# The first stage of a hybrid decoder trunk: x in its own places, the second half by blocks, the rotary tables early

## The chip, the core and the metric

The kernel runs on one core of a Trainium2 chip. The metric is the time of one execution on the device in microseconds, as a median of several runs; lower is better. The core has TensorE (matrix products, PE in the rows), VectorE (DVE), ScalarE (ACT), GpSimd (POOL), and SyncE (SP), whose queue issues all DMAs here. Each takes its instructions in a fixed order and waits on semaphores.

## The reference

Two layers over 1024 tokens of width 1024. The first layer's mixer begins with an RMS norm and one input projection; 512 of its columns go to a causal pooling (two groups of 128 channels, and their gates), the others to six heads of differential attention with a partial rotary embedding.

```python
hn = rmsnorm(h, norm_g[i])
z = hn @ w_in
a_in, a_gate, q, k, v, b_gate = split(z)
a = multiscale_pool(a_in)          # trailing means over 2, 4, 8, 16 tokens, minus the token
a = einsum(a, pool_w) * pool_scale * silu(a_gate)
q = partial_rope(rmsnorm(q, q_norm), positions, 16, 500000.0)     # k likewise
o = diff_attention(q, k, v, lam)
h = h + concat([a, o]) @ w_out
```

The second layer has latent attention and a gated delta rule. Each layer ends with a gated addition of per-layer inputs. All of that is the same before and after.

## The kernel before, in words

Activations lie transposed: 8 blocks k of 128 channels, 2 halves h of 512 tokens. To multiply float32 at the fast rate each operand is split into a rounded high part and a low rest (`split`, L131); a product is then three matmuls (`mm3`, L141, lines L142, L143, L144). The norm's gain `ng` scales x as it is split (L137 on ScalarE for the high part, L138 on VectorE for the low one); the norm's 1/rms comes in later, as a row over tokens (`rrow`).

The first stage (L343 to L366) loads x and the pooling's 512 weight columns. `load_x` (L312) takes one x block into a raw buffer (four raw buffers serve x and weights alike), splits it, and lets ScalarE square it and GpSimd add the squares (L322). The first half is multiplied block by block into four PSUM banks; the weights are rounded on VectorE (L349) and the rest is taken there (L350). Then the constants are loaded, `finish_x` (L324) makes 1/rms: column sums on TensorE (L182), a root by Newton steps on VectorE (L111 to L116), a row by a product with ones (`token_row`, L185, operand at L187, product L190, copy L191). `pool_in` (L334) takes the banks out. After it the second half's eight x blocks are loaded and split, and multiplied column block by column block. The rotary tables (`rope_tables`, L193; called at L370) are a chain of some 60 small VectorE operations (L207 to L227), two sines on ScalarE (L228) and copies on GpSimd.

Then come the projections of head 0 (`even_proj`, L433; weights split on ScalarE L134 and VectorE L135) and between them the pooling (`even_pool`, L407): shifted sums on GpSimd (L411), and on VectorE, for each half of the partitions, a scaling and subtraction (L422 to L424). Its product is L428.

The code is written in a program order, but a scheduler decides at build time in which order each engine's queue holds the instructions; it lets work that is ready early move ahead. Before the change it had moved much of the tables' chain between the first half and the last three x blocks. Pools of tiles with a tag hand out their buffers in turn; an instruction that needs a buffer still in use waits.

Of the kernel before, what the change touches and what calls it, by code (L numbers as in the profile page):

```python
# [10 lines left out]
F32 = mybir.dt.float32  # L11
F32R = mybir.dt.float32r
I32 = mybir.dt.int32
# [8 lines left out]
P = 128  # L22
# [34 lines left out]
def trunk_kernel(ctx, tc, a, out, layers=2):  # L57
# [11 lines left out]
    def nm(p):  # L69
        uid[0] += 1  # L70
        return f"{p}{uid[0]}"
# [76 lines left out]
        dma.dma_start(raw, src)  # L148
        return raw

    def wload(ap, c0, n, nk=KC):

        res = []
        for k in range(nk):
            raw = wp.tile([P, 512], F32, tag="raw", bufs=4, name=nm("raw"))[:, :n]
            hi = wp.tile([P, 512], F32R, tag="hi", name=nm("wh"))[:, :n]
            lo = wp.tile([P, 512], F32R, tag="lo", name=nm("wl"))[:, :n]
            dma.dma_start(raw, ap[k * P:(k + 1) * P, c0:c0 + n])
            split(hi, lo, raw)
            res.append((hi, lo))  # L160
        return res
# [31 lines left out]
    def rope_tables(pool, lo, n, tmp, tab=None):  # L193
# [1 line left out]

        posi = pool.tile([P, NT], I32, name=nm("posi"))
        dma.dma_start(posi, a["positions"].rearrange("b (t p) -> p (b t)", p=P))
        posf = pool.tile([P, NT], F32, name=nm("posf"))  # L200
        v.tensor_copy(posf, posi)
        ct, st = [(tab or pool.tile)([P, NT, 2 * n], F32, name=nm(i)) for i in ("cos", "sin")]
        acc = st.rearrange("p t n -> p (t n)")[:, 0:NT * n]
        fr = ct.rearrange("p t n -> p (t n)")[:, 0:NT * n]
# [100 lines left out]
    yp = pools["sm"] = pools["y"]  # L305
    PW, PBUFS = [T_ + 16], {0: 2, 1: 1}

    ng = vec(cp, "ng", a["norm_g"].rearrange("l (c p) -> p (l c)", p=P), 16)
    hn = [[None, None] for _ in range(KC)]
    rrow = [T("g", 3) for _ in range(2)]  # L310

    def load_x(h, k, sums):  # L312
        raw = stage(a["xT"][k * P:(k + 1) * P, h * 512:(h + 1) * 512])
        hi, lo = xt(), xt()
        split(hi, lo, raw, ng[:, k:k + 1])
        hn[k][h] = (hi, lo)
        if k == 0:
            s.activation(sums, raw, AF.Square)
        else:
            sq = T("z", 2)  # L320
            s.activation(sq, raw, AF.Square)
            g.tensor_tensor(out=sums, in0=sums, in1=sq, op=ALU.add)  # L322
# [17 lines left out]
        s.activation(th, ag, AF.Tanh, scale=0.5)  # L340
        v.scalar_tensor_tensor(out=ag, in0=th, scalar=1.0, in1=ag, op0=ALU.add, op1=ALU.mult)

    sums = T("o", 2)  # L343
    first, w_pool = [bank(n) for n in ("acc", "acc", "s", "s")], []
    for k in range(KC):
        load_x(0, k, sums)
        raw = stage(a["ev_w_in"][k * P:(k + 1) * P, 0:512])
        hi, lo = [wp.tile([P, 512], F32R, tag=n, name=nm(n)) for n in ("hi", "lo")]
        v.tensor_copy(hi, raw)  # L349
        v.tensor_tensor(out=lo, in0=raw, in1=hi.bitcast(F32), op=ALU.subtract)  # L350
        w_pool.append((hi, lo))
        for j in range(4):
            q = slice(j * P, j * P + P)
            mm3(first[j], hi[:, q], lo[:, q], *hn[k][0], k == 0, k == KC - 1)
    dma.dma_start(cst, a["cst"])
    finish_x(0, sums)
    for j in range(4):
        pool_in(first[j], j, 0)
    sums = T("o", 2)
    for k in range(KC):  # L360
        load_x(1, k, sums)
    finish_x(1, sums)
    for j, n in enumerate(("x", "x", "tr", "acc")):
        ps = bank(n)
        proj_T(hn, w_pool, j, 1, ps)
        pool_in(ps, j, 1)  # L366

    rtmp = T("o", 2, (3, 64))
    rtmp = [rtmp[:, i, :] for i in range(3)]
    cos0, sin0 = rope_tables(yp, 0, 8, lambda dt: rtmp.pop().bitcast(dt),  # L370
                             lambda shape, dt, name: T("pt", 2, shape[1:], dt))
    lvt = T("o", 2)[:, 0:256]
    dma.dma_start(lvt, a["ev_lambda"].rearrange("o a b -> (o a b)").partition_broadcast(P))
    neglam = yp.tile([P, 1], F32, name="neglam")
# [32 lines left out]
    def even_pool(b):  # L407
        x, s2, s4 = px[b], T("p0", 2, (L,)), T("p0", 2, (L,))

        def shift_add(dst, src, sh, lo):  # L410
            g.tensor_tensor(out=dst[lo:P, sh:L], in0=src[lo:P, sh:L], in1=src[lo:P, 0:L - sh], op=ALU.add)  # L411
            g.memset(dst[lo:P, 0:sh], 0.0)

        g.memset(x[:, 0:16], 0.0)
        shift_add(s2, x, 1, 0)
        shift_add(s4, s2, 2, 64 if b == 0 else 0)
        if b == 1:
            shift_add(s2, s4, 4, 0)
            shift_add(s4, s2, 8, 64)
        for sw, lo in ((s2, 0), (s4, 64)):  # L420
            q = slice(lo, lo + 64)
            v.tensor_tensor(out=sw[q, 16:32], in0=sw[q, 16:32], in1=cst[q, C_ICNT + 16 * b:C_ICNT + 16 * b + 16], op=ALU.mult)  # L422
            v.tensor_tensor(out=x[q, 16:32], in0=sw[q, 16:32], in1=x[q, 16:32], op=ALU.subtract)
            v.scalar_tensor_tensor(out=x[q, 32:L], in0=sw[q, 32:L], scalar=cst[q, C_IW + b:C_IW + b + 1],  # L424
                                   in1=x[q, 32:L], op0=ALU.mult, op1=ALU.subtract)
        for h in range(2):
            pm = bank("s")
            pe.matmul(pm, pw[:, b, :], x[:, 16 + 512 * h:528 + 512 * h], start=True, stop=True)  # L428
            ct = T("sq", 3)
            v.scalar_tensor_tensor(out=ct, in0=pm, scalar=pscale[:, b:b + 1], in1=pg[2 * b + h], op0=ALU.mult, op1=ALU.mult)  # L430
            dma.dma_start(cat[0][b][h], ct)
# [883 lines left out]
```

## Time and profile before

| | |
|---|---|
| median of 3 runs (lowest, highest) | 1497.71 us (1496.02, 1498.46) |
| the profiled execution's own time | 1490.0 us |
| its span, first to last instruction | 1488.3 us |
| TensorE busy | 1419.7 us, 95% of the span |
| VectorE busy | 1000.5 us, 67% |
| ScalarE, GpSimd busy | 655.7 us, 44%; 206.2 us, 14% |
| mean granted TensorE clock | 0.99 of full speed |
| DMA | 181.52 MB, 122 GB/s in the mean |

The busy share is a mean over stages. TensorE's slices show 7 in the first and fourth slot and nearly always 9 behind them, so the stage at the start is looked at by itself below. Every time of an instruction is from the one profiled execution.

### The profile page before, as it was taken

To read this page: it belongs to the slowest core of one execution; us is meant where nothing else is said; L and a number is where in the kernel's file an instruction comes from. 1 tells how busy PE (TensorE), PEld (TensorE's weight loads), DVE (VectorE), ACT (ScalarE), POOL (GpSimd) and SP (SyncE) were. 2 spreads that over 40 slices of the span, in tenths; PEclk is the share of its full clock that TensorE was granted. 3 is DMA by queue.
4 is the path that set the end of the run, shared out by engine and by line. 5 is a ranking of instruction groups with operands and counts; after the bars stand their busy time and mean duration, and the time that the engine had idled before them with its cause. 6 is when DMAs were issued, how large, how long until landed. Compare 5 with 4: busy or idle time off the path is not lost. (4 is left out here: it accounts for less than half of the span.)

```text
span 1488.3 us, 22788 instructions
## 1 busy us (share of the span) xinstructions
PE 1419.7 (95%) x7494; PEld 1158.3 (78%) x7494; DVE 1000.5 (67%) x2939; ACT 655.7 (44%) x1642; POOL 206.2 (14%) x347
## 2 busy tenths in 40 slices
PE   7799999999999999999998999999889999999998
PEld 6578887888888778887886777888768788887786
DVE  7855666676767857356669789888577888643342
ACT  4415555565566751234454434444223446722220
POOL 3430101010101001012104441110000000000021
PEclk9999999999999999999999999999989999999999
DMA  5315233232335483334323442343455644353332
GB/s 166 95 51 141 56 101 79 78 90 68 100 86 148 134 276 94 107 120 152 118 41 131 167 154 99 99 133 123 138 162 183 212 140 149 114 156 99 120 114 85
DMA packets 131557, 181.52 MB, mean 122 GB/s; under 512 B 32496, under 2 KB 59248, under 8 KB 131440
## 3 DMA queue, kind: packets, MB, share of 16 engines
q1 hardware_dynamic: 131440, 180.08, 39.7%
q8 instruction: 59, 0.97, 0.3%
q14 instruction: 58, 0.48, 0.1%
HBM read 108.20 MB, written 52.95 MB: 108 GB/s over the span
## 5 line engine op out<-in xcount | busy, mean ns | idle before, releaser
L142 PE MATMUL acc<-wh,x 128*128 128x512 f32 (+1 forms) x576 | 231.6, 402 | 2.3 <-DVE g L454 1.9
L143 PE MATMUL acc<-wl,x 128*128 128x512 f32 (+1 forms) x576 | 229.9, 399 | 3.0 <-DVE wl L135 3.0
L144 PE MATMUL acc<-wh,x 128*128 128x512 f32 (+1 forms) x576 | 228.5, 397 | 0.0
L144 PE MATMUL acc<-x,wl 128*128 128x512 f32 x512 | 204.5, 400 | 3.3 <-DVE wl L135 3.3
L142 PE MATMUL acc<-x,wh 128*128 128x512 f32 x512 | 204.8, 400 | 1.9 <-ACT wh L134 0.9
L143 PE MATMUL acc<-x,wh 128*128 128x512 f32 x512 | 203.0, 397 | 0.0
L134 ACT CAST wh<-raw 128x512 fp32r<-128x512 f32 (+2 forms) x176 | 101.3, 599 | 80.2 <-PE acc L143 25.6
L135 DVE TENSOR_TENSOR wl<-raw,wh 128x512 fp32r<-128x512 f32 (+2 forms) x176 | 114.9, 674 | 28.6 <-ACT wh L134 25.9
L143 PEld LDWEIGHTS acc<-wl,x 128*128 128x128 f32 x576 | 109.4, 190 | 27.1 <-DVE wl L135 4.5
L142 PEld LDWEIGHTS acc<-wh,x 128*128 128x128 f32 x576 | 109.3, 190 | 25.7 <-issue 2.8
L144 PEld LDWEIGHTS acc<-wh,x 128*128 128x128 f32 x576 | 109.2, 190 | 22.3
L144 PEld LDWEIGHTS acc<-x,wl 128*128 128x128 f32 x512 | 96.5, 188 | 27.9 <-DVE wl L135 5.9
L142 PEld LDWEIGHTS acc<-x,wh 128*128 128x128 f32 x512 | 96.4, 188 | 25.0 <-ACT wh L134 1.3
L265 ACT ACTIVATE p<-p,mx 128x128 f32<-128x128 f32 (+7 forms) x128 | 99.4, 777 | 33.0 <-DVE mx L261 24.3
L143 PEld LDWEIGHTS acc<-x,wh 128*128 128x128 f32 x512 | 96.3, 188 | 21.5
L669 POOL TENSOR_TENSOR u<-hp,hp 128x512 f32<-128x512 f32 x32 | 43.5, 1358 | 486.9 <-DVE hp L135 205.7
L144 PE MATMUL acc<-hp,wl 128*128 128x512 f32 x256 | 101.6, 397 | 0.4 <-DVE wl L135 0.4
L143 PE MATMUL acc<-hp,wh 128*128 128x512 f32 x256 | 101.5, 396 | 0.0
L142 PE MATMUL acc<-hp,wh 128*128 128x512 f32 x256 | 101.4, 396 | 0.0
L261 DVE CUSTOM_DVE_ANT_0 p<-s,cst 128x512 f32<-128x512 f32 (+3 forms) x128 | 74.2, 586 | 29.2 <-PE s L523 15.6
L667 DVE SCALAR_TENSOR_TENSOR th<-th,ld 128x512 f32<-128x512 f32 x32 | 28.8, 899 | 73.7 <-ACT th L665 73.7
L450 ACT ACTIVATE z<-acc,rstd 128x256 f32<-128x256 f32 x48 | 22.7, 474 | 112.2 <-PE acc L144 112.2
(462 smaller groups left out, 2906.1 us busy)
## 6 DMA issues: line engine op xcount, KB each, us to landing
raw<-in_ev_w_in SPq DMA_DIRECT2D x56, 256.0 KB
Q<-sq SPq DMA_DIRECT2D x96, 128.0 KB
qkv<-zz SPq DMA_DIRECT2D x16, 640.0 KB
raw<-cat SPq DMA_DIRECT2D x32, 256.0 KB
ple<-z SPq DMA_DIRECT2D x32, 256.0 KB
raw<-in_ple_w_gate SPq DMA_DIRECT2D x32, 256.0 KB
ld<-ple SPq DMA_DIRECT2D x32, 256.0 KB
zq<-qkv SPq DMA_DIRECT2D x16, 512.0 KB
```

The source lines that it names most:

```text
L134: s.copy(hi, src)
L135: v.tensor_tensor(out=lo, in0=src, in1=hi.bitcast(F32), op=ALU.subtract)
L142: pe.matmul(ps, lh, rh, start=first, stop=False)
L143: pe.matmul(ps, lh, rl, start=False, stop=False)
L144: pe.matmul(ps, ll, rh, start=False, stop=last)
L261: v.tensor_tensor_reduce(out=pm[:, c * 512:c * 512 + n], in0=ps[:, 0:n], in1=mk, scale=-scale, scalar=prev, op0=ALU.add, op1=ALU.min, accu ...
L265: s.activation(pm[:, 0:w], pm[:, 0:w], AF.Exp, bias=prev, scale=-1.0, accum_out=sums)
L450: s.activation(z[:, t % 4, :], ps[:, 0:256], AF.Identity, scale=rstd[0][:, t:t + 1])
L667: v.scalar_tensor_tensor(out=th, in0=th, scalar=1.0, in1=r, op0=ALU.add, op1=ALU.mult)
L669: g.tensor_tensor(out=u, in0=hi.bitcast(F32), in1=lo.bitcast(F32), op=ALU.add)
```

## The change

- The gains and the positions are loaded as rows and turned by one transpose into `npos` (128x48), from which `ng` and `posf` are views; the identity part of the constants is loaded first, the rest in two later parts.
- x goes into tiles that later hold head 0's K, V and probabilities (`slots`), not into the raw buffers.
- The weights of the first stage are loaded by `wload`, one block per call, so that the high part is rounded on ScalarE (L134).
- The rotary tables are called in the first half's loop, behind block 1.
- The second half is multiplied block by block into three banks as it is split; the fourth column block follows when a bank of `acc` is free. `finish_x(0)` is called behind block 2, and the banks of the first half are taken out from block 4 on.
- `even_pool` copies the lower 64 partitions to the other tile on ScalarE and then scales and subtracts all 128 at once.

```diff
--- before
+++ after
-    def wload(ap, c0, n, nk=KC):
+    def wload(ap, c0, n, nk=KC, row=0):
         res = []
-        for k in range(nk):
+        for k in range(row, row + nk):
...
-        posi = pool.tile([P, NT], I32, name=nm("posi"))
-        dma.dma_start(posi, a["positions"].rearrange("b (t p) -> p (b t)", p=P))
-        posf = pool.tile([P, NT], F32, name=nm("posf"))
-        v.tensor_copy(posf, posi)
...
-    ng = vec(cp, "ng", a["norm_g"].rearrange("l (c p) -> p (l c)", p=P), 16)
+    dma.dma_start(ident, a["cst"][:, C_ID:C_ID + P])
+    rows, posi = T("rt", 1, (P,)), T("th", 2, (P,), I32)[0:NT]
+    v.memset(rows[0:64], 0.0)
+    dma.dma_start(rows[32:48], a["norm_g"].rearrange("l (c p) -> (l c) p", p=P))
+    dma.dma_start(posi, a["positions"].rearrange("b (t p) -> (b t) p", p=P))
+    v.tensor_copy(rows[0:NT], posi)
+    npos = cp.tile([P, 48], F32, name="npos")
+    ps = bank("tr")
+    pe.transpose(ps[:, 0:64], rows[0:64], ident[0:64, 0:64])
+    v.tensor_copy(npos, ps[:, 0:48])
+    posf, ng = npos[:, 0:NT], npos[:, 32:48]
...
+    slots = [[t[:, i, :] for t in [T("K", 4, (2, 512)) for _ in range(4)] for i in range(2)],
+             [T("v", 4) for _ in range(4)] + [t[:, 512 * i:512 * i + 512] for t in [T("p0", 2, (PW[0],)) for _ in range(2)] for i in range(2)]]
     def load_x(h, k, sums):
-        raw = stage(a["xT"][k * P:(k + 1) * P, h * 512:(h + 1) * 512])
+        raw = slots[h][k]
+        dma.dma_start(raw, a["xT"][k * P:(k + 1) * P, h * 512:(h + 1) * 512])
...
-    sums = T("o", 2)
+    sums = [T("o", 2) for _ in range(2)]
     first, w_pool = [bank(n) for n in ("acc", "acc", "s", "s")], []
     for k in range(KC):
-        load_x(0, k, sums)
-        raw = stage(a["ev_w_in"][k * P:(k + 1) * P, 0:512])
-        hi, lo = [wp.tile([P, 512], F32R, tag=n, name=nm(n)) for n in ("hi", "lo")]
-        v.tensor_copy(hi, raw)
-        v.tensor_tensor(out=lo, in0=raw, in1=hi.bitcast(F32), op=ALU.subtract)
-        w_pool.append((hi, lo))
+        load_x(0, k, sums[0])
+        w_pool += wload(a["ev_w_in"], 0, 512, row=k, nk=1)
         for j in range(4):
             q = slice(j * P, j * P + P)
-            mm3(first[j], hi[:, q], lo[:, q], *hn[k][0], k == 0, k == KC - 1)
-    dma.dma_start(cst, a["cst"])
-    finish_x(0, sums)
-    for j in range(4):
-        pool_in(first[j], j, 0)
-    sums = T("o", 2)
-    for k in range(KC):
-        load_x(1, k, sums)
-    finish_x(1, sums)
-    for j, n in enumerate(("x", "x", "tr", "acc")):
-        ps = bank(n)
-        proj_T(hn, w_pool, j, 1, ps)
-        pool_in(ps, j, 1)
-    rtmp = T("o", 2, (3, 64))
-    rtmp = [rtmp[:, i, :] for i in range(3)]
-    cos0, sin0 = rope_tables(yp, 0, 8, lambda dt: rtmp.pop().bitcast(dt),
-                             lambda shape, dt, name: T("pt", 2, shape[1:], dt))
+            mm3(first[j], w_pool[k][0][:, q], w_pool[k][1][:, q], *hn[k][0], k == 0, k == KC - 1)
+        if k == 1:
+            dma.dma_start(cst[:, C_INVF:C_END], a["cst"][:, C_INVF:C_END])
+            rtmp = T("g", 3, (3, 64))
...
+            cos0, sin0 = rope_tables(yp, 0, 8, ...)
+    second = [bank(n) for n in ("x", "x", "tr")]
+    dma.dma_start(cst[:, P:C_INVF], a["cst"][:, P:C_INVF])
+    for k in range(KC):
+        load_x(1, k, sums[1])
+        for j in range(3):
+            q = slice(j * P, j * P + P)
+            mm3(second[j], w_pool[k][0][:, q], w_pool[k][1][:, q], *hn[k][1], k == 0, k == KC - 1)
+        if k == 2:
+            finish_x(0, sums[0])
+        if k > 3:
+            pool_in(first[k - 4], k - 4, 0)
+    finish_x(1, sums[1])
+    second.append(bank("acc"))
+    proj_T(hn, w_pool, 3, 1, second[3])
     for j in range(4):
+        pool_in(second[j], j, 1)
...
-        for sw, lo in ((s2, 0), (s4, 64)):
-            q = slice(lo, lo + 64)
-            v.tensor_tensor(out=sw[q, 16:32], in0=sw[q, 16:32], in1=cst[q, ...], op=ALU.mult)
-            v.tensor_tensor(out=x[q, 16:32], in0=sw[q, 16:32], in1=x[q, 16:32], op=ALU.subtract)
-            v.scalar_tensor_tensor(out=x[q, 32:L], in0=sw[q, 32:L], scalar=cst[q, ...], in1=x[q, 32:L], ...)
+        s.copy(s4[0:64, 16:L], s2[0:64, 16:L])
+        v.tensor_tensor(out=s4[:, 16:32], in0=s4[:, 16:32], in1=cst[:, ...], op=ALU.mult)
+        v.tensor_tensor(out=x[:, 16:32], in0=s4[:, 16:32], in1=x[:, 16:32], op=ALU.subtract)
+        v.scalar_tensor_tensor(out=x[:, 32:L], in0=s4[:, 32:L], scalar=cst[:, ...], in1=x[:, 32:L], ...)
```

How the scheduler's order moves. First, VectorE's queue where the first half is split; before (`x` are the parts of x, `hi` and `lo` of the weights):

```order
L138 SCALAR_TENSOR_TENSOR x_278<-raw_275,ng,x_277 128x512
L349 CAST hi_286<-raw_284 128x512
L350 TENSOR_TENSOR lo_287<-raw_284,hi_286 128x512
L138 SCALAR_TENSOR_TENSOR x_305<-raw_302,ng,x_304 128x512
L349 CAST hi_313<-raw_311 128x512
L350 TENSOR_TENSOR lo_314<-raw_311,hi_313 128x512
```

and after (`wl` is the low part of a weight block, `g` and `pt` are the tables' work tiles):

```order
L138 SCALAR_TENSOR_TENSOR x_359<-K_172,npos,x_358 128x512
L213 SCALAR_TENSOR_TENSOR pt_241<-g_240 128x64
L135 TENSOR_TENSOR wl_367<-raw_365,wh_366 128x512
L217 TENSOR_TENSOR pt_242<-pt_242,pt_241 128x64
L212 TENSOR_SCALAR g_240<-g_240 128x64
L138 SCALAR_TENSOR_TENSOR x_385<-K_172,npos,x_384 128x512
```

The cast has left the queue, and three operations of the tables stand in each block. Second, TensorE's queue around the first row product L190; before:

```order
L142 MATMUL x_515<-x_456,hi_286 128x512
L143 MATMUL x_515<-x_457,hi_286 128x512
L190 MATMUL o_406<-sq_404,cst 128x512
L144 MATMUL x_515<-x_456,lo_287 128x512
L142 MATMUL x_541<-x_422,hi_178 128x512
```

and after:

```order
L144 MATMUL x_461<-x_557,wl_367 128x512
L190 MATMUL o_536<-sq_534,cst 128x512
L142 MATMUL x_462<-x_557,wh_366 128x512
L143 MATMUL x_462<-x_558,wh_366 128x512
L144 MATMUL x_462<-x_557,wl_367 128x512
```

In both it stands in the second half behind block 4; before, that was within the first column block, and after it is within the loop that multiplies three column blocks at a time; 33 products of that loop stand behind it. Third, VectorE's queue at the head of the first half's root (`tokm` to `newton`), which makes that product's operand; before:

```order
L138 SCALAR_TENSOR_TENSOR x_457<-raw_454,ng,x_456 128x512
L121 TENSOR_SCALAR tokm_389<-o_384 128x4
L207 TENSOR_SCALAR o_625<-cst,posf_628 128x8
L111 TENSOR_SCALAR toky_391<-tokm_389 128x4
L207 TENSOR_SCALAR o_625<-cst,posf_628 128x8
L113 TENSOR_TENSOR newton_392<-toky_391 128x4
```

and after:

```order
L222 TENSOR_TENSOR g_240<-g_240 128x64
L223 TENSOR_SCALAR g_240<-g_240 128x64
L135 TENSOR_TENSOR wl_738<-raw_736,wh_737 128x512
L121 TENSOR_SCALAR tokm_519<-o_514 128x4
L111 TENSOR_SCALAR toky_521<-tokm_519 128x4
L113 TENSOR_TENSOR newton_522<-toky_521 128x4
```

Before, the root began behind the fifth x block of the second half, together with the first step of the tables. After, all eight x blocks, the tables to their end and the first weight block of head 0 stand ahead of it. From the first product of head 0 on, TensorE's order is the same in both.

## Rows read from the trace of the kernel before

**Rows 1.** Windows: us, busy of PE, PEld, DVE, ACT, POOL, clock, DMA, GB/s.

```profile
11.40:32.20 20.80, 20.80 (x91) 16.75 (x90) 19.07 (x23) 9.70 (x17) 8.91 (x6) 1.00 0.65 190
...
47.90:55.10 7.20, 0.36 (x2) 0.00 (x0) 6.92 (x15) 3.08 (x6) 4.58 (x4) 0.81 0.11 34
...
55.10:59.70 4.60, 4.57 (x12) 3.61 (x13) 3.26 (x12) 0.91 (x2) 0.00 (x0) 0.55 0.58 164
...
92.30:97.00 4.70, 4.70 (x14) 3.70 (x15) 1.26 (x3) 0.00 (x0) 0.00 (x0) 0.64 0.30 113
```

**Rows 2.** TensorE's timeline, start: start, duration, instruction, idle before, releaser.

```profile
7.34 0.76 PE L142 MATMUL acc<-x,hi 128*128 128x512 f32 x1 [7.34 <-DVE hi L349]
8.64 0.79 PE L143 MATMUL acc<-x,hi 128*128 128x512 f32 x1 [0.53 <-DVE x L138]
...
9.66 0.63 PE L142 MATMUL acc<-x,hi 128*128 128x512 f32 x1
10.09 0.63 PE L143 MATMUL acc<-x,hi 128*128 128x512 f32 x1
```

**Rows 3.** TensorE's timeline, 28 to 100 us.

```profile
32.18 0.95 PE L182 MATMUL o<-cst,o 128*128 128x1 f32 x8
...
55.13 0.79 PE L143 MATMUL x<-x,hi 128*128 128x512 f32 x1 [6.87 <-DVE x L138]
...
67.39 1.10 PE L190 MATMUL o<-sq,cst 128*128 128x512 f32 x2 [1.77 <-DVE neglam L381]
...
70.88 0.40 PE L142 MATMUL acc<-wh,x 128*128 128x512 f32 x1
...
92.26 0.47 PE L142 MATMUL acc<-wh,x 128*128 128x512 f32 x1 [1.91 <-DVE g L454]
```

**Rows 4.** VectorE's timeline, 20 to 60 us.

```profile
22.10 0.42 DVE L349 CAST hi<-raw 128x512 fp32r<-128x512 f32 x1
...
26.59 1.52 DVE L349 CAST hi<-raw 128x512 fp32r<-128x512 f32 x1
...
28.14 0.69 DVE L350 TENSOR_TENSOR lo<-raw,hi 128x512 fp32r<-128x512 f32 x1
28.75 0.74 DVE L138 SCALAR_TENSOR_TENSOR x<-raw,ng,x 128x512 fp32r<-128x512 f32 x1
...
43.36 1.28 DVE L216 TENSOR_SCALAR o<-o 128x64 int32<-128x64 f32 x1
...
52.72 0.18 DVE L216 TENSOR_SCALAR o<-o 128x64 int32<-128x64 f32 x1
...
53.34 0.19 DVE L216 TENSOR_SCALAR o<-o 128x64 int32<-128x64 f32 x1
...
54.33 0.75 DVE L138 SCALAR_TENSOR_TENSOR x<-raw,ng,x 128x512 fp32r<-128x512 f32 x1
...
55.49 0.75 DVE L138 SCALAR_TENSOR_TENSOR x<-raw,ng,x 128x512 fp32r<-128x512 f32 x1
```

**Rows 5.** VectorE's timeline, the pooling.

```profile
86.16 3.41 DVE L424 SCALAR_TENSOR_TENSOR Q<-p,cst,Q 64x1008 f32<-64x1008 f32 x1
...
89.78 1.27 DVE L424 SCALAR_TENSOR_TENSOR Q<-p,cst,Q 64x1008 f32<-64x1008 f32 x1
```

**Rows 6.** GpSimd's timeline, and its group in 7.31 to 57.4 us (count, busy, mean).

```profile
43.22 9.50 POOL L322 TENSOR_TENSOR o<-o,z 128x512 f32<-128x512 f32 x7 [15.40 <-ACT z L321]
...
L322 POOL TENSOR_TENSOR o<-o,z 128x512 f32<-128x512 f32 x14 | 19.6, 1402 | 31.8 <-ACT z L321 31.4
```

**Rows 7.** ScalarE's and SP's timelines, first stage.

```profile
4.99 1.28 ACT L137 ACT_TABLE_LOAD   x1 [4.99 <-DMA raw<-in_xT]
...
50.60 0.60 ACT L134 CAST wh<-raw 128x512 fp32r<-128x512 f32 x1
...
1.30 1.40 SPq L148 DMA_DIRECT2D raw<-in_xT  x1
```

**Rows 8.** Waits of ScalarE, 0 to 60 us: total, times, longest.

```profile
ACT x L137 <- DMA raw<-in_xT: 13.0, 10, 2.5
```

More of the change, by code (lines that the diff above doesn't have):

```diff
@@ L368, in trunk_kernel @@
-    rtmp = T("o", 2, (3, 64))
-    rtmp = [rtmp[:, i, :] for i in range(3)]
-    cos0, sin0 = rope_tables(yp, 0, 8, lambda dt: rtmp.pop().bitcast(dt),
-                             lambda shape, dt, name: T("pt", 2, shape[1:], dt))
+            mm3(first[j], w_pool[k][0][:, q], w_pool[k][1][:, q], *hn[k][0], k == 0, k == KC - 1)
+        if k == 1:
+            dma.dma_start(cst[:, C_INVF:C_END], a["cst"][:, C_INVF:C_END])
+            rtmp = T("g", 3, (3, 64))
+            rtmp = [rtmp[:, i, :] for i in range(3)]
+            cos0, sin0 = rope_tables(yp, 0, 8, lambda dt: rtmp.pop().bitcast(dt),
+                                     lambda shape, dt, name: T("pt", 2, shape[1:], dt))
@@ L419, in even_pool @@
             shift_add(s4, s2, 8, 64)
-        for sw, lo in ((s2, 0), (s4, 64)):
-            q = slice(lo, lo + 64)
-            v.tensor_tensor(out=sw[q, 16:32], in0=sw[q, 16:32], in1=cst[q, C_ICNT + 16 * b:C_ICNT + 16 * b + 16], op=ALU.mult)
-            v.tensor_tensor(out=x[q, 16:32], in0=sw[q, 16:32], in1=x[q, 16:32], op=ALU.subtract)
-            v.scalar_tensor_tensor(out=x[q, 32:L], in0=sw[q, 32:L], scalar=cst[q, C_IW + b:C_IW + b + 1],
-                                   in1=x[q, 32:L], op0=ALU.mult, op1=ALU.subtract)
+        s.copy(s4[0:64, 16:L], s2[0:64, 16:L])
+        v.tensor_tensor(out=s4[:, 16:32], in0=s4[:, 16:32], in1=cst[:, C_ICNT + 16 * b:C_ICNT + 16 * b + 16], op=ALU.mult)
+        v.tensor_tensor(out=x[:, 16:32], in0=s4[:, 16:32], in1=x[:, 16:32], op=ALU.subtract)
+        v.scalar_tensor_tensor(out=x[:, 32:L], in0=s4[:, 32:L], scalar=cst[:, C_IW + b:C_IW + b + 1],
+                               in1=x[:, 32:L], op0=ALU.mult, op1=ALU.subtract)
         for h in range(2):
```

## The prediction, as it was made before the changed kernel ran

> **What bounds the kernel now.** I read the page first: TensorE is busy for 95% of the span, VectorE for 67%. A stage before the dense part can therefore gain only what TensorE idles or runs slowly in it. Second came the windows over the first 140 us [rows 1]: from 11.4 to 32.2 us TensorE has no gap and takes 20.80/91 = 0.23 us a product of 128x512; from 47.9 to 55.1 us it has work for 0.36 us; after that gap it runs at a granted clock of 0.55 for 4.6 us, with 12 products where 20 would fit at 0.23 us, a loss of 8 x 0.23 = 1.9 us. Third came TensorE's timeline. The first product starts at 7.34 us, the second at 8.64 us; the start runs at the lower level, one product per 10.09 - 9.66 = 0.43 us [rows 2]. Later gaps: 6.87 us until VectorE's low part of an x block, 1.77 us before the row product L190, and 1.91 us at 92.26 us until VectorE's L454 [rows 3]. The first product of head 0 starts at 70.88 us. That is the number that I forecast anew; from there on the order of TensorE's work is the same.
>
> Fourth came VectorE's own rows, since it ends the longest gap. Between 43.36 and 52.72 us it does nine small operations, three rounds of three; the next round, free of it, takes 53.34 - 52.72 = 0.62 us. So 9.36 us hold 1.9 us of work [rows 4]. In that time GpSimd runs seven sums of squares without a pause [rows 6]. Each costs VectorE (9.36 - 1.9)/7 = 1.07 us. ScalarE waits 13.0 us in ten pieces for x to land [rows 8], but TensorE is covered then. So the stage is bound by TensorE until 47 us, then by VectorE, which GpSimd holds up.
>
> **The change part by part.** *The start.* The gather of norm_g in single elements goes; behind it the issue of the first x block took 1.40 us [rows 7]. In its place stand a memset, for which SP's queue waits with all x loads behind it, two short loads by rows, a conversion, a transpose and a copy, and only then can ScalarE scale x. The trace shows no such transpose here; the chain is worth between 0, if it ends while x is still landing, and 2 us, if it begins only when x lands at 5 us. I take the first: with three short issues ahead of x and the 1.40 us gone, x lands about when it did, and ScalarE does the square first. The table load, which waited for x until 4.99 us and took 1.28 us [rows 7], has no wait now. ScalarE then has square, scaling and the cast (0.60 us) [rows 7] before the first product: I put it at 7.4 us, as now. The 0.53 us pause and the slow second product [rows 2] go, a gain that the VectorE sum below swallows.
>
> *The casts.* Eight leave VectorE (0.42 us free, 1.52 us when a sum of GpSimd lies across it) [rows 4] for ScalarE. ScalarE was busy for 9.70 of 20.80 us [rows 1], 1.3 us per block of 12 x 0.23 = 2.8 us; with a cast it is 1.9 us. So they cost nothing there.
>
> *The rotary tables* move from the gap to between the splits. 47 of their operations stand between the splits of all 16 x blocks now instead of in front of the last three, and the tail of the tables, one weight split and the whole chain of the first half's rstd stand ahead of the operand of the first L190. In TensorE's order that L190 stands after block 4 of the second half, with 33 products of the second half behind it. So TensorE can't pass until VectorE has done everything up to that operand. ScalarE's exponential for lambda, which needs a later load, stands ahead of the copy of that row product; it may hold the copy up by 1 to 2 us, but TensorE has 7.6 us of products before it needs what hangs on it.
>
> VectorE's sum from 8.1 us (its first two splits done): 15 splits of x at 0.66 (1.16 from one to the next with a round of three between them, less 0.50), 9.9; 7 weight splits at 28.75 - 28.14 = 0.61, 4.3 [rows 4]; 8 products of position and frequency and 18 table operations of the first half, at 0.50/3 = 0.17 at most, and at 0.135 as I take it, since a big one now lies between most of those that wait for each other, 3.5; 7 rounds in the second half at 0.50, 3.5; the dependent tail and two small scalings, 11 at about 0.2, 2.0; the wait for ScalarE, which does a sine and a cast ahead of the weight split behind the tables, 1.0, and that split, 0.6; the rstd chain, 12 dependent small ones at 0.62/3 = 0.21, 2.5, and L187, 0.6. Together 27.9 us. Add 13 of the 14 sums of GpSimd (one comes later) at 1.07, 13.9, and 0.7 for GpSimd's eight small table products beside the chain. End: 8.1 + 27.9 + 13.9 + 0.7 = 50.6 us.
>
> TensorE alone would be there at 7.4 + 8 x 0.43 + 127 x 0.23 + 0.8 (the column sums L182, 0.95 in their row [rows 3], less what the next product covers) = 41 us. x no longer waits for a raw buffer, so ScalarE and GpSimd run ahead and take VectorE's turns early; pauses of about 3 us in the first half are likely, but they fit into these 9 us.
>
> From 50.6 us: L190, 0.9 (1.10 in its row less overlap); 33 products, 7.6; L182, 0.8; 24 products of the last column block, 5.5; the second L190, 0.9; a wait before it of 0.6, since the rstd chain now runs between four weight splits that need freed buffers (it is 1.77 now) [rows 3]; and 1.9 for the lower clock after the wait, as in [rows 1]. Sum 18.2, so head 0 starts at 68.8 us: 2.1 us earlier.
>
> *The pooling.* Two passes over 64 partitions become one over 128 and a ScalarE copy. A pass of 1008 columns takes 1.27 us free and 3.41 us when GpSimd holds it up [rows 5]; I assume that as many columns cost the same on 128 partitions (bounds: 1.27 and twice that). The copy of 64x1024 is in no row; by the 128x512 cast it lies between 0.6 and 1.2 us, and it runs while GpSimd does the other window. Per window VectorE saves 1.3 to 3.4 us, which ends the release of a bank that TensorE awaits at 92.26 us. I work out a rest of 0.4 of the 1.91 us: gain 1.5. The dip behind it, 4.70 us at 0.64 [rows 1], holds 14 products that take 3.2 us: gain 1.5, if no pause brings it back. Together 3.0 us.
>
> One rule speaks against this. Measured, a sum on GpSimd costs VectorE 1.07 us, while the mean sum takes 1.40 us [rows 6]. The Trainium skill, SBUF — State Buffer, "Who interferes with whom", says that the loser blocks until the other has finished: by that a sum would cost its full length, 13 x 0.33 = 4.3 us more than mine. I keep the row, since VectorE's end and GpSimd's beginning overlap there.
>
> *At nothing:* the positions that layer 1 no longer loads (one small cast); loads of the constants in three parts, beside the x stream; the later SP issues, which are ahead of their use.
>
> Sum: -2.1 - 3.0 = -5.1 us on the profiled 1490.0 us, so 1484.9. The median of the timed runs is 1497.71, 7.7 us above that one execution; I carry the difference over: 1492.6 us.
>
> **The rivals.**
> 1. *VectorE doesn't bind.* If GpSimd's sums fall where VectorE waits anyway, TensorE runs through: 7.4 + 192 x 0.23 + 1.6 for the slow first eight + 2 x 1.7 + 0.6 = 57.2 us, 13.7 earlier, with the pooling -16.7: 1481.0 us. For it: ScalarE runs ahead. Against: VectorE is busy for 19.07 of 20.80 us in a stretch where it does as much per block [rows 1].
> 2. *The gap only moves.* Each sum holds VectorE for its whole 1.40 us, or the rstd chain is longer by as much: head 0 starts at 73.1 us, 2.2 later, and the pooling gives 3.0: -0.8, 1496.9 us. For it: the cast of 0.42 us that met a sum took 1.52 us [rows 4]. That is the page's rule above.
> 3. *Slower: the clock doesn't rise.* Because ScalarE and GpSimd run ahead, VectorE feeds the first half in pieces, and TensorE pauses in every block. A product at the lower level costs 0.43 - 0.23 = 0.20 us more. TensorE has 50.6 - 41 = 9.6 us to give before L190, that is 48 slow products of 127; from 48 on each moves the end. With all 127, L190 comes at 66.4 and the kernel ends 15.8 - 5.1 = 10.7 us later: 1508.4. For it: the pause of 1.91 us was followed by 4.70 us at 0.64. Against: the clock was up after four microseconds of products without a gap (1.00 from 11.4 us) [rows 1], and the first two blocks are still fed without one.
>
> **How the numbers follow.** Forecast 0.50, rival 1 0.14, rival 2 0.23, rival 3 0.13. Two kernels of this length can be told apart from about 0.2%, 3.0 us. The forecast's own range is 1489 to 1496: of its 0.50, 0.41 is faster by more than that and 0.09 not. Rival 1 is faster; rival 2 is no change but for 0.02 on each side; rival 3 is slower with 0.10 and no change with 0.03, since half of its price may be hidden. That gives faster 0.57, same 0.31, slower 0.12. The range for 8 in 10 is 1485 to 1501: it leaves out most of rival 1 and the upper half of rival 3, and takes in 0 to 2 us for the chain at the start and 0.6 to 1.2 for the copy.
>
> **What would show it.** Right: the first product near 7.4 us; small table operations of 1 us and more between 9 and 45 us; TensorE waiting at the first L190 for VectorE until about 50 us, a low clock behind it, head 0 from about 69 us; one 128x1008 pass per window, and less than 1 us of pause near 90 us. Wrong: head 0 before 62 us (rival 1) or after 72 us (rivals 2 and 3; a granted clock near 0.6 from 11 to 35 us is rival 3), a ScalarE copy that GpSimd delays so that an eviction of `acc` comes late, or a kernel that loses after 100 us what it gained before.

## The result, and the profile after

| | before | after |
|---|---|---|
| median (lowest, highest), taken together | 1496.87 us (1492.54, 1498.46), 4 executions | 1483.48 us (1482.08, 1484.62), 4 executions |
| ratio | | 0.9915, 95% interval 0.9892 to 0.9938 |
| the profiled execution's own time, span | 1490.0, 1488.3 us | 1483.52, 1481.8 us |

The changed kernel is faster, by 0.85%. From profile to profile it gained 6.5 us where 5.1 were forecast. The median of 1483.48 lies 9.1 us under the forecast of 1492.6 and under its range. So the stage went much as forecast, and the way from the profile to the median did not.

First the windows of the changed kernel that answer to [rows 1] (columns as there).

```profile
11.40:32.20 20.80, 20.04 (x86) 15.86 (x85) 20.80 (x33) 16.18 (x28) 18.38 (x10) 1.00 0.63 206
47.90:55.10 7.20, 5.58 (x11) 3.80 (x12) 4.62 (x16) 1.68 (x4) 0.14 (x1) 0.50 0.17 42
55.10:59.70 4.60, 4.60 (x20) 3.65 (x20) 1.48 (x2) 0.90 (x2) 1.29 (x1) 0.94 0.00 0
92.30:97.00 4.70, 4.70 (x18) 3.16 (x17) 2.60 (x7) 1.51 (x4) 0.00 (x0) 1.00 0.14 56
```

TensorE's slices show 8 in the first two slots, where before they show 7 in the first and the second (not the fourth, which has 9). The first half is still fed nearly without a gap (20.04 of 20.80 us), while VectorE, ScalarE and GpSimd are all fuller. The clock is at its lower level from 48 to 55 us, behind the wait, and in the last window it is at 1.00 with 18 products, where before it was 0.64 with 14. Next TensorE's timeline of the changed kernel, against [rows 2, 3].

```profile
3.63 0.36 PE L313 MATMUL tr<-cst,rt 64*128 64x64 f32 x1 [3.63 <-DVE rt L310]
6.63 1.22 PE L142 MATMUL acc<-x,wh 128*128 128x512 f32 x2 [2.63 <-ACT wh L134]
...
29.77 0.50 PE L144 MATMUL acc<-x,wl 128*128 128x512 f32 x1 [0.76 <-DVE wl L135]
...
49.52 2.05 PE L190 MATMUL o<-sq,cst 128*128 128x512 f32 x2 [6.90 <-DVE sq L187]
...
66.95 1.10 PE L190 MATMUL o<-sq,cst 128*128 128x512 f32 x2
...
68.57 0.39 PE L142 MATMUL acc<-wh,x 128*128 128x512 f32 x1
...
87.59 0.48 PE L142 MATMUL acc<-wh,x 128*128 128x512 f32 x1 [0.37 <-DVE g L465]
```

One wait is left, 6.90 us for the operand of the first row product. Head 0 starts at 68.57 instead of 70.88 us, and the pause in the pooling is 0.37 instead of 1.91 us. Then ScalarE's start.

```profile
0.81 1.28 ACT L329 ACT_TABLE_LOAD   x1 [0.81 <-PEq L1316]
4.83 0.63 ACT L329 ACTIVATE o<-K 128x512 f32<-128x512 f32 x1 [2.74 <-DMA K<-in_xT]
5.36 0.70 ACT L137 ACTIVATE x<-K,npos 128x512 fp32r<-128x512 f32 x1
5.97 0.60 ACT L134 CAST wh<-raw 128x512 fp32r<-128x512 f32 x1
```

The table load no longer waits for x (0.81 instead of 4.99 us in [rows 7]). The transpose L313 is done at 4 us, before x lands at 4.8 us, so the new chain at the start costs nothing. Last VectorE's timeline, against [rows 4, 5].

```profile
14.68 1.32 DVE L212 TENSOR_SCALAR g<-g 128x64 int32<-128x64 f32 x1
...
17.32 1.33 DVE L215 COPY pt<-pt 128x64 f32<-128x64 f32 x1
18.57 0.18 DVE L212 TENSOR_SCALAR g<-g 128x64 int32<-128x64 f32 x1
18.67 0.73 DVE L138 SCALAR_TENSOR_TENSOR x<-K,npos,x 128x512 fp32r<-128x512 f32 x1
...
29.78 1.78 DVE L138 SCALAR_TENSOR_TENSOR x<-v,npos,x 128x512 fp32r<-128x512 f32 x1
...
45.54 0.81 DVE L135 TENSOR_TENSOR wl<-raw,wh 128x512 fp32r<-128x512 f32 x1 [0.83 <-ACT wh L134]
46.27 0.15 DVE L121 TENSOR_SCALAR tokm<-o 128x4 f32<-128x4 f32 x1
...
48.69 0.69 DVE L187 TENSOR_TENSOR sq<-cst,rstd 128x512 f32<-128x512 f32 x1
...
76.96 1.25 DVE L435 SCALAR_TENSOR_TENSOR p<-p,cst,p 128x1008 f32<-128x1008 f32 x1
...
85.25 1.26 DVE L435 SCALAR_TENSOR_TENSOR Q<-p,cst,Q 128x1008 f32<-128x1008 f32 x1
```

The same L212 takes 0.18 us free and 1.32 us where a sum of GpSimd lies across it. From 8.1 us to the one that begins at 39.43 us there are 13 operations lengthened in this way (two of them an L138), one for each of the 13 sums. The pass of 1008 columns over 128 partitions takes 1.25 us, as one over 64 did.

### The profile page after: what moved, and what is told of

Same layout as the page of the kernel before. It is cut to its first block, busy times and chain, and to the rows that moved or that the text cites. A ratio compares the mean times of both kernels' runs of the same rounds, so it can differ in the third digit from the quotient of the medians.

```text
span 1481.8 us, 22778 instructions
## 1 busy us (share of the span) xinstructions
PE 1420.4 (96%) x7495; PEld 1157.4 (78%) x7495; DVE 988.9 (67%) x2926; ACT 662.1 (45%) x1652; POOL 212.6 (14%) x347
## 3 DMA queue, kind: packets, MB, share of 16 engines
q1 hardware_dynamic: 127632, 180.08, 39.8%
## 5 line engine op out<-in xcount | busy, mean ns | idle before, releaser
L142 PE MATMUL acc<-wh,x 128*128 128x512 f32 (+1 forms) x576 | 230.6, 401 | 0.6 <-DVE g L465 0.4
L142 PE MATMUL acc<-x,wh 128*128 128x512 f32 x536 | 215.8, 403 | 4.5 <-ACT wh L134 3.2
L144 PE MATMUL acc<-x,wl 128*128 128x512 f32 x536 | 214.0, 400 | 4.0 <-DVE wl L135 4.0
L143 PE MATMUL acc<-x,wh 128*128 128x512 f32 x536 | 212.5, 397 | 0.0
L134 ACT CAST wh<-raw 128x512 fp32r<-128x512 f32 (+2 forms) x184 | 106.8, 600 | 81.2 <-PE acc L143 37.5
L135 DVE TENSOR_TENSOR wl<-raw,wh 128x512 fp32r<-128x512 f32 (+2 forms) x184 | 120.7, 674 | 28.9 <-ACT wh L134 27.2
L142 PEld LDWEIGHTS acc<-wh,x 128*128 128x128 f32 x576 | 108.5, 189 | 24.2 <-PE acc L144 0.8
L144 PEld LDWEIGHTS acc<-x,wl 128*128 128x128 f32 x536 | 101.3, 189 | 30.4 <-DVE wl L135 7.1
L142 PEld LDWEIGHTS acc<-x,wh 128*128 128x128 f32 x536 | 101.0, 189 | 29.5 <-ACT wh L134 4.0
L143 PEld LDWEIGHTS acc<-x,wh 128*128 128x128 f32 x536 | 101.2, 189 | 22.4 <-issue 0.2
L142 PE MATMUL acc<-hp,wh 128*128 128x512 f32 x256 | 101.5, 396 | 0.0
L257 DVE CUSTOM_DVE_ANT_0 p<-s,cst 128x512 f32<-128x512 f32 (+3 forms) x128 | 74.1, 585 | 29.4 <-PE s L534 15.4
```

Source lines behind the costliest of these rows:

```text
L134: s.copy(hi, src)
L135: v.tensor_tensor(out=lo, in0=src, in1=hi.bitcast(F32), op=ALU.subtract)
L142: pe.matmul(ps, lh, rh, start=first, stop=False)
L143: pe.matmul(ps, lh, rl, start=False, stop=False)
L144: pe.matmul(ps, ll, rh, start=False, stop=last)
L257: v.tensor_tensor_reduce(out=pm[:, c * 512:c * 512 + n], in0=ps[:, 0:n], in1=mk, scale=-scale, scalar=prev, op0=ALU.add, op1=ALU.min, accu ...
```

## The experiments

**Repeats and parts, on one chip.** (Each later set of runs is from another chip; every ratio is to executions of the kernel before beside it.) Theory A: the stage and the pooling gain what the profiles show, and medians of three or four executions are draws from a wide scatter. Theory B: the timed executions run in another way than the profiled one.

The kernel before, unchanged.

> The kernel before once more, unchanged, with a new profile. Theory A (the extra 7 us are a matter of which executions were drawn): its times lie between 1490 and 1499 us as before, the ratio to itself is 1.000, and its new profile puts head 0 at 70.9 us within 0.5. Theory B (executions of the kernel before differ in one place that the change removed): the times fall into two groups some 6 to 8 us apart, and a slow profile shows one pause or one stretch of low clock that the first profile lacked; in the changed kernel it can't occur.

1494.2 us, 1.0004 (0.9987 to 1.0021) of the 35 executions beside it, which had a median of 1494.33 and went from 1487.05 to 1500.02. Head 0 starts at 71.02 us in the new profile, as expected.

The changed kernel, unchanged.

> The changed kernel once more. Both theories: 1482 to 1485 us, L190 first at 49.5 us. Theory A: before is drawn at 1490 to 1493 in the mean beside it and the gain is 6 to 9 us; theory B: the gain stays 12 to 14 us.

1486.08 us (1482.53 to 1492.99), 0.9947 (0.9928 to 0.9966). The median is 1.1 us above the range expected. With more executions the gain is 8 us, as theory A has it, and the first three of before stand near the top of their scatter.

The new first stage alone:

```diff
-        s.copy(s4[0:64, 16:L], s2[0:64, 16:L])
...
+        for sw, lo in ((s2, 0), (s4, 64)):    # the four passes of 64 partitions, as before
```

> The new first stage with the old pooling in two passes of 64 partitions. By the sums of the prediction head 0 starts at 68 to 69 us, 2 to 3 us earlier than before, and the pause of 1.9 us near 88 us and the low clock behind it come back: 3.0 to 3.6 us more than the changed kernel. Theory B, if the place that varies lies in the first stage: this kernel has the narrow spread of the changed one; if it lies in the pooling: the wide one.

1490.22 us, 0.9976 (0.9953 to 0.9998). Its TensorE timeline in the pooling:

```profile
89.32 0.50 PE L142 MATMUL acc<-wh,x 128*128 128x512 f32 x1 [2.29 <-DVE g L466]
```

Head 0 starts at 68.11 us, and the pooling's pause stays, as expected; the lower clock behind it does not come back. Windows of the kernel before, first and second profile, around the same pause (1.91 and 1.93 us):

```profile
90.00:96.00 6.00, 4.09 (x13) 3.01 (x12) 3.53 (x7) 0.99 (x3) 0.00 (x0) 0.78 0.23 89
```

```profile
90.00:96.00 6.00, 4.07 (x18) 2.98 (x18) 3.66 (x7) 0.99 (x3) 0.00 (x0) 1.00 0.23 89
```

So the pause is there in both, and the dip of the clock in one only. (It comes again in the profiles of before with filling, below: 0.83 and 0.80 in this window.) From the first product of head 0 to its first transpose it takes 41.6 us with the dip and 40.0 without it in the kernel before, 39.8 with the new stage alone, and 37.6 and 37.9 in the two profiles of the changed kernel so far. Behind the new stage the new pooling is thus worth about 2 us.

The new pooling alone (the same edit in the kernel before, the other way round).

> The old first stage with the new pooling in one pass of 128 partitions. By the sums: head 0 at 70.9 us as before, the pause near 92 us under 0.5 us, 3.0 to 3.6 us less than the kernel before in profiles. Theory B: wide spread if the place that varies lies in the first stage.

1492.36 us, 0.9996 (0.9975 to 1.0016). Its TensorE timeline:

```profile
78.12 0.50 PE L143 MATMUL acc<-wl,x 128*128 128x512 f32 x1 [2.10 <-DVE wl L135]
```

The pause near 92 us is gone, but TensorE waits as long at 78 us for a weight split, and head 0 takes 41.0 us to its first transpose. So the pooling's term is real only behind the new stage: alone it moves the wait. The 3.0 to 3.6 us expected of it in profiles did not come (this profile's span is 1494.3 us; most of the 6.0 us that it is longer than the first come after 680 us, far from the edit). By the times, the parts give 0.24% and 0.04%, together 0.53%; with intervals of 0.2% each way these do not show whether the parts add up.

**The wait of 6.9 us.** The tables called behind the second half's loop:

```diff
-        if k == 1: ... cos0, sin0 = rope_tables(...)      # in the first half's loop
+    cos0, sin0 = rope_tables(...)                         # behind the second half's loop
```

> The call that computes the rotary tables is moved from behind block 1 of the first half to behind the loop of the second half; all else is as in the changed kernel. Theory 1 (VectorE's queue, lengthened by the tables and by GpSimd's sums that block their small operations, ends the wait of 6.9 us before the first L190): the operand of L190 is ready some 9 us earlier, TensorE waits there for less than 1 us, at 42 to 43 us, the granted clock stays at 1.00 behind it, head 0 starts at 59 to 61 us instead of 68.2, and the kernel is 6 to 9 us shorter than the changed one. Theory 2 (the chain of the root, or the x blocks alone, end that wait, with or without the tables): L190 stays later than 47 us and the time stays within 2 us of the changed kernel's. Theory 3 (the gap only moves): L190 is early, but the tables then hold up VectorE ahead of the weight splits of head 0, TensorE waits there instead, and head 0 or its first ten products come no more than 3 us earlier.

1485.05 us (1481.16 to 1488.03), 0.9941 (0.9922 to 0.9960). TensorE's timeline of this kernel, then VectorE's:

```profile
41.40 1.10 PE L190 MATMUL o<-sq,cst 128*128 128x512 f32 x2
...
57.63 0.39 PE L142 MATMUL acc<-wh,x 128*128 128x512 f32 x1
...
66.76 0.50 PE L143 MATMUL acc<-wl,x 128*128 128x512 f32 x1 [2.91 <-DVE wl L135]
```

```profile
62.10 3.89 DVE L352 SCALAR_TENSOR_TENSOR Q<-z,Q 128x512 f32<-128x512 f32 x2 [0.76 <-ACT z L351]
65.92 0.18 DVE L206 TENSOR_SCALAR g<-g 128x64 int32<-128x64 int32 x1
66.02 0.68 DVE L135 TENSOR_TENSOR wl<-raw,wh 128x512 fp32r<-128x512 f32 x1
```

No wait at L190 and head 0 eleven us earlier: theory 1 holds for the wait. About 5 of the eleven come back in three pauses by 89 us (theory 3 in part): 2.91 us at 66.76 us, where VectorE's L352 takes nearly 2 us each beside GpSimd's pooling sums and a weight split comes late, and 0.60 and 1.33 us before L142 at 80.06 and 88.94 us. The gain of 6 to 9 us did not come in the time: the changed kernel beside it has 1484.12 us.

GpSimd's additions left out:

```diff
-            g.tensor_tensor(out=sums, in0=sums, in1=sq, op=ALU.add)
+            pass
```

> GpSimd's 14 additions of the squares of x are left out (each half's sum of squares holds its first block alone); all else is as in the changed kernel, the tables in their early place. Theory 1 (each addition blocks one small VectorE operation for about 1.07 us): VectorE's small table operations take 0.2 us instead of 1.3, the operand of L190 is ready 10 to 14 us earlier, TensorE waits at L190 less than 1 us, at 42 us, and head 0 starts near 60 us; the kernel is 6 to 9 us shorter than the changed one. Rival (the long operations come from VectorE's own dependences or from waits for ScalarE, and GpSimd's additions only happen beside them): the same operations still take over 1 us and L190 comes at 47 us or later. If both this kernel and the one with the late tables come to the same head-0 start, the stage is bound by TensorE in both.

1478.56 us, 0.9907 (0.9871 to 0.9943). VectorE's timeline, then TensorE's:

```profile
11.58 0.20 DVE L212 TENSOR_SCALAR g<-g 128x64 int32<-128x64 f32 x1
11.68 0.75 DVE L138 SCALAR_TENSOR_TENSOR x<-K,npos,x 128x512 fp32r<-128x512 f32 x1
```

```profile
41.90 1.10 PE L190 MATMUL o<-sq,cst 128*128 128x512 f32 x2
```

No VectorE operation takes over 0.9 us between 8 and 45 us, and TensorE does not wait at L190. So GpSimd's sums, through VectorE's small table operations, make the wait. That was argued in the prediction and is shown here. Head 0 starts at 58.12 us, within 0.5 us of the kernel with late tables, as the expectation had it for a stage that TensorE binds in both. The time is 5.6 us below that of the changed kernel beside it, a little less than the 6 to 9 expected, from four executions.

The changed kernel a third time:

> The changed kernel unchanged, beside the two others on one chip, so that their gains can be read against it. If medians of few runs are draws from a scatter of about 6 us each way, it comes to 1483 to 1489 us and to 0.9925 to 0.9965 of the kernel before; a median outside that would mean that chips or occasions differ by more than executions do.

1484.12 us (1480.90 to 1490.19), 0.9942 (0.9922 to 0.9962), as expected. Its profiled execution settled more: its span is 1487.9 us, 6.1 longer than that of the first profile of the very same kernel. Up to 1097 us it is even 0.7 us ahead. Then, in windows, the first profile of the changed kernel and this one:

```profile
1101.00:1118.00 17.00, 15.33 (x155) 12.00 (x156) 11.59 (x57) 4.86 (x13) 0.83 (x2) 0.83 0.67 203
```

```profile
1101.00:1118.00 17.00, 16.00 (x90) 11.72 (x91) 8.89 (x43) 2.92 (x9) 0.30 (x1) 0.50 0.64 196
```

In the same 17 us one does 155 products at a mean clock of 0.83, the other 90 at 0.50, the lower level. The stretch begins in a wait that the profile of every kernel without filling has; TensorE's timeline of the third run:

```profile
1097.35 0.44 PE L1155 MATMUL s<-K,Q 128*128 128x384 f32 x1 [1.71 <-DVE mx L257]
...
1102.00 0.79 PE L268 MATMUL o<-V,pt 128*128 128x128 f32 x2 [3.45 <-DVE r L1163]
```

What ends the wait is a store of layer 2 (`gate`): VectorE's L257 stands idle until it lands, here in the first profile of the changed kernel, and the product behind it waits in turn.

```profile
1101.37 0.42 DVE L257 CUSTOM_DVE_ANT_0 p<-s,cst 128x256 f32<-128x256 f32 x1 [3.42 <-DMA gate<-gz]
```

By the trace's record of the granted clock TensorE then stays at the lower level for 6.8 us in the first profile and for 23.9 us in the third run's. The time from that L1155 (L1144 in the kernel before) to the end of the span comes in two values. It is 382.4, 382.8, 383.0, 383.3, 383.8 and 384.7 us in the profiles of before, of before again, of the changed kernel again, of the pooling alone, of the changed kernel and of the one without sums. It is 390.5, 390.6, 390.6 and (below) 392.0 in those of the stage alone, of the late tables, of the third run and of the control.

The timed executions carry the mean granted clock of each. I cut them at 0.988, seeing the two groups:

| | clock 0.988 and more | below |
|---|---|---|
| before, 113 executions | 61, median 1491.6 (1487.1 to 1495.6) | 52, median 1497.4 (1494.5 to 1500.9) |
| changed, 24 executions | 14, median 1483.5 (1480.9 to 1486.2) | 10, median 1489.9 (1488.0 to 1493.0) |

The change is worth 8.1 us in one group and 7.5 in the other. Which group an execution falls into moves it by 6 us. So there are two groups, as theory B had it, but in both kernels, so that the draw decides, as theory A had it. The cut fits these two kernels: a kernel that loses other dips of the clock has a higher mean with the same stretch. The one with late tables lacks the dip of the first stage, and its profiled execution, with 23.9 us at the lower level, has 0.989.

**Filling the wait.** Needless products in that wait, the same edit in each kernel; 16 first, then 10. So that they stay ahead of the scan's products, the scan's steps begin two steps later.

```diff
+        for _ in range(fill):       # hd == 0 and i == 0 only; the product behind overwrites it
+            pe.matmul(ps, pm[:, 0:P], ident, start=True, stop=True)
         product(*last)
...
-            step(at, rec)
+            step(at, *([rec] if hd or i > 1 else []))
```

> The changed kernel, with TensorE given 16 needless products of 128x128 in the wait of 3.4 us near 1099 us (into the bank that the product behind them overwrites; the steps of the scan begin two steps later so that they stay behind them). In two profiles of the changed kernel with the same instructions the clock was granted at half for 6.8 us from there (span 1481.8) and for 23.9 us (span 1487.9). Theory S (that wait starts the stretch at half clock, and its length, which differs from one execution to the next, makes two groups of times, 1481 to 1484 and 1488 to 1490): with the wait filled the granted clock stays at 1.00 near 1100 us or falls for 3.4 us at most, the upper group is gone, the timed executions lie within 4 us of each other but for single ones, and the median is 1478 to 1482. Theory C (the long stretch comes to the chip at about that time, whatever TensorE does there): two groups about 6 us apart remain, and the median stays at 1483 to 1487.

> The kernel before with the same filling of the same wait (3.5 us near 1107 us). Theory S: its upper group (1494 to 1500) goes too, the median is 1484 to 1489, that is 6 to 12 us below the median of the kernel before, and the difference between this kernel and the filled changed one is what the two profiles differ by, 5.5 to 8 us. Theory C: two groups remain, and the median stays above 1491.

> The changed kernel with the steps of the scan begun two steps later, and no needless products: the control for the other two. If the delay by itself does nothing, it has the changed kernel's two groups and its median, 1483 to 1487. If the delay takes the wait away, the idle time ahead of the product near 1102 us falls under 2 us and this kernel is as fast as the filled one.

> The kernel with the late rotary tables, with the same filling. Its profile was 6 to 7 us ahead of the changed kernel's up to 1095 us and lost that in one stretch of 23.9 us at half clock. Theory S: with the wait filled it is 4 to 8 us faster than the filled changed kernel, 1472 to 1477. Theory C: it stays at 1481 to 1486.

Measured: changed with 16, 1486.67 us (1483.47 to 1494.79), 0.9951 (0.9933 to 0.9969); before with 16, 1497.57 us, 1.0020 (1.0003 to 1.0037); the delay alone, 1490.34 us, 0.9978 (0.9959 to 0.9997); late tables with 16, 1480.41 us (1478.19 to 1481.35), 0.9906 (0.9883 to 0.9928). All three filled kernels miss the times that theory S expected, the executions of the changed and the before kernel spread over 11 us instead of 4, and the control lies above its range too. TensorE's timeline of the changed kernel with 16 says part of why:

```profile
1097.61 5.37 PE L282 MATMUL o<-cst,p 128*128 128x128 f32 x32
```

They take 5.37 us where the wait was 3.4, so they cost time of their own; so does the delay, whose kernel has both groups (6 of 12 below 0.988) and a wait of 3.12 us. What theory S says of the clock held: the stretch is 3.4 us in the profiles of all three. With 10:

> The changed kernel with 10 needless products in the wait near 1099 us instead of 16. 16 took 5.37 us, 10 should take 3.4 us and end with the wait. Theory S (the long stretch starts in that wait and makes the upper group): no execution has a mean clock under 0.988, and the median is 1480 to 1484, at or a little under the lower group of the changed kernel (1481 to 1484). Theory C: groups 6 us apart remain, or the median stays at 1486 or more although the products fit.

> The kernel before with 10 needless products in the same wait. Theory S: at most one execution in ten has a mean clock under 0.988, the median is 1487 to 1492, in or under the lower group of the kernel before (1487 to 1494), and its distance to the filled changed kernel is 5.5 to 9 us. With 16 products it was 10.9 us; if it stays above 9.5 us here, the filling costs the kernel before something that the changed one doesn't pay, and the two can't be compared in this way.

> The kernel with late tables with 10 needless products in the same wait. It was 1480.4 us with 16. If the shorter filling saves its 1.7 us, the median is 1476 to 1480, and this version is faster than the changed kernel (1484 to 1486) by 5 us or more.

Measured: changed 1483.89 us (1481.97 to 1486.67), 0.9932 (0.9912 to 0.9953); before 1492.53 us (1489.94 to 1496.02), 0.9982 (0.9967 to 0.9997); late tables 1478.48 us (1476.50 to 1479.58), 0.9894 (0.9872 to 0.9916). All are as expected, but for the median of before, 0.5 us above its range. TensorE's timeline of the first, then its window:

```profile
1097.41 3.72 PE L282 MATMUL o<-cst,p 128*128 128x128 f32 x20
1101.39 0.59 PE L268 MATMUL o<-V,pt 128*128 128x128 f32 x2 [0.26 <-ACT pt L277]
```

```profile
1101.00:1118.00 17.00, 16.50 (x186) 13.62 (x186) 12.37 (x62) 5.54 (x15) 1.14 (x3) 0.98 0.73 223
```

With the wait filled, 186 products fit into the window at 0.98. In the profile of before with 10 the clock does not fall there at all. Over the three kernels with 10 no execution of 24 is below 0.988, with 16 it is 2 of 30 (both of before); of the unfilled before, changed and control kernels 68 of 149. So the wait starts the long stretch (theory S), and the upper group is that stretch. The filled medians lie by the lower groups (1483.9 and 1483.5; 1492.5 and 1491.6): the filling takes the long stretch away and gains nothing beyond that. The gain between the two kernels, both without it, is 8.6 us. Against the control, which has the delay alone and ran on another chip, the filling is worth 0.46% by the two ratios. Filled, the late tables are 5.4 us ahead of the changed kernel: this version beats both kernels. Unfilled their lead did not show in the median. Like with like it does: with the long stretch in both, the profile of the late tables has a span of 1481.8 us, that of the changed kernel's third run 1487.9. How many of the nine unfilled executions had the long stretch is not known, since the cut does not serve for this kernel. What makes the stretch long in one execution and short in the next stays open.

## Why the prediction was wrong, and where it was right

**The step that failed** is the last: "The median of the timed runs is 1497.71, 7.7 us above that one execution; I carry the difference over". The difference is no constant of the kernel. It is the long stretch at the lower clock near 1105 us, which 46% of the executions of before have and the profiled one had not. The three runs that gave 1497.71 were by their times all of the upper group (1496.02 and more, where the lower one ends at 1495.6); the four of the changed kernel were all of the lower (1484.62 and less, clock 0.990 and more). The medians of the first result (before with a fourth execution, 1492.54) differ by 13.4 us, of which the change is 8 and the draw the rest. The forecast of 1484.9 for an execution like the profiled one stands against 1483.52 measured. The sum of -5.1 us was itself too small beside the 7.5 to 8.6 us that like executions differ by; the profiles show 6.3 us of them by the first transpose of head 0, and where the rest lies is open. Rival 1's 1481.0 lies nearer to the measured median, but its mechanism did not come: TensorE waited 6.90 us at L190. Rival 3 did not come either, the clock was 1.00 from 11.4 to 32.2 us; its counter-argument overlooks the pause of 0.53 us in the prediction's own [rows 2], since the products ahead of 11.4 us were not without a gap.

| step | forecast | measured |
|---|---|---|
| first product | 7.4 us | 6.63 |
| TensorE at the first L190 | 41 us | 42.6 |
| operand there, wait | 50.6, 9 us | 49.52, 6.90 |
| from there to head 0 | 18.2 us | 19.05 |
| head 0 starts | 68.8 us (-2.1) | 68.57 (-2.3) |
| pooling | -3.0 us | -4.0 |
| after the pooling | nothing | -0.2 |

The measured column is from one profile of each kernel, and profiles of one kernel differ by about 2 us between the pooling and the wait near 1099 us. That head 0 came within 0.2 us of the forecast is in part luck: the operand of L190 was 1.1 us earlier than put, and the way from there 0.9 us longer.

*The start:* x landed as forecast and the transpose was done before. ScalarE's three operations then ran from 4.83 to 6.57 us, the table load being done before them, and the first product came 0.8 us earlier than put. *The casts* cost nothing on ScalarE, as put, but for 0.83 us at 45.54 us where VectorE waits for one (1.0 was put in). *The tables:* 13 sums at 1.07 were put at 13.9 us. Measured, L212 loses 1.32 - 0.18 = 1.14 us to a sum and L138 1.78 - 0.73 = 1.05, so between 13.7 and 14.8 us. The Trainium skill ("SBUF — State Buffer", "Who interferes with whom") says that the loser waits for the whole instruction of the other; the trace agrees nearly, as a sum alone takes 1.29 us here (GpSimd's row at 39.42 us). This decided nothing. Pauses of 3 us in the first half were expected; one of 0.76 came. *The second wait* of 0.6 before the second L190 did not come; the lower clock behind the first wait, still 0.50 from 47.9 to 55.1 us, cost more than the 1.9 us put in, and 18.2 became 19.05. *The pooling:* the pause went to 0.37 as forecast (0.4) and the clock stayed up (1.00). The transposes of head 0 start at 106.2 instead of 112.5 us, 6.3 earlier, of which 2.3 were there when head 0 began. Of the 4.0 us, 1.54 are that pause, 0.48 a pause in head 0's first column block that the sum had overlooked, and about 1.5 the dip of the clock, as put. But the term is not the pooling's own, as its run alone showed, and the dip is no fixed price of the pause: the kernel before again had the same pause without it and was 1.5 us faster there. That it stood in the profile that the forecast used, and not in the one after, was luck. Against the new stage alone, without a dip, the new pooling is worth about 2 us, not 4.

The chances were right in sign: faster. The range was drawn about the carried median, and so it missed.

## What to carry to other kernels

Before a profile's gain is added to a timed median, look at whether the profiled execution and the median are of the same kind: the mean granted clock of each execution shows it, and a stage that may run 7 us longer at the lower clock is a term of its own, not an offset. A wait of 3.4 us in a dense stage was followed by up to 23.9 us at half speed; needless products that fit into the wait took the slower group of executions away, and ones that overran it cost what they gave. A dip of the clock behind a pause in one profile is not yet a price of that pause: look for it in a second profile. And an edit that removes a wait should be tried with its neighbour, since alone it may only move the wait to the next operand in the queue.

## What the runs showed of the hardware

- The same instructions behind the same wait ran at the lower clock for 6.8 us in some executions and for 23.9 in others, although TensorE had products throughout (busy for 16.00 of 17 us). The same pause of 1.9 us near 92 us was followed by the lower clock in three profiles of the kernel before (two of them with the later filling) and not in the fourth.
- On VectorE an operation with one input of 128x64 (L212, 0.18 us) loses as much to a sum of GpSimd as a two-input split of 128x512 (0.73 us): 1.14 and 1.05 us. GpSimd can lose as much: in a row of sums beside VectorE four take 10.11 us, while one by itself takes 1.29:

```profile
14.14 10.11 POOL L333 TENSOR_TENSOR o<-o,z 128x512 f32<-128x512 f32 x4 [0.17 <-ACT z L332]
...
39.42 1.29 POOL L333 TENSOR_TENSOR o<-o,z 128x512 f32<-128x512 f32 x1
```

- A needless float32 product of 128x128 counts as two matmul records. Ten took 2.40 us at a clock of 1.00 (before with 10), 0.24 us each, as much as a product of the split parts with 512 columns (0.23). Ten took 3.72 us in the changed kernel, where the clock fell to 0.50 while they ran. TensorE's timeline of before with 10:

```profile
1109.64 2.40 PE L286 MATMUL o<-cst,p 128*128 128x128 f32 x20
```
